# A two-layer hybrid decoder: the first loads go out on two queues, and the last four weight steps take the first 128 tokens ahead of the second 128

## The chip, the cores and the metric

One NeuronCore of one Trainium2 chip runs the whole program. The metric is the time of one execution in microseconds, as the device measures it; the profile of one such execution has a span (first to last instruction) that is a little shorter. Engines are named as the profile names them: PE (TensorE, PEld is its weight loading), DVE (VectorE), ACT (ScalarE), POOL (GpSimd) and SP (SyncE, which here only issues loads and stores). Each engine works through its own list of instructions in order: one that waits for a semaphore holds up all that is behind it on that engine.

## What is computed

The input x is 256 tokens of 1024 features in float32. Two layers follow, and a final norm:

```
for l in range(2):
    h = rms_norm(x, norm_mix_w[l]);  z = h @ w_in[l] + b_in[l]          # 1024 x 5640
    ya = dilated_mixture_attention(rope(aq), rope(ak), av)              # columns of z
    yb = sigmoid(mo) * rms(mlstm(silu(conv(mq, mk)), mv, mi, mf))       # columns of z
    x = x + (sigmoid(ga) * (ya @ w_proj_att[l]) + sigmoid(gb) * (yb @ w_proj_mlstm[l])) @ w_out[l]
    x = x + square(relu(rms_norm(x, norm_mlp_w[l]) @ w_ff1[l])) @ w_ff2[l]
out = rms_norm(x, final_norm_w)
```

## The kernel before, in words

**Weight steps.** All weights are read once, in steps of 256 rows by 512 columns (512 KB). SP loads a step into one of six buffers `raw`. ACT rounds it to a shorter mantissa (`hi`, five buffers), DVE subtracts (`lo` = raw - hi), and PE multiplies activations and weights as three products: low activation by hi, high activation by hi, high activation by lo. The activations are kept the same way, as `slot0h`, `slot0l` (and `slot1h`, `slot1l`). PE results go to eight PSUM tiles `bank`. The products of a step are written either by feature (`by_feature`, 128x256) or by token (`by_token`, 128x512).

**Order.** The program's order is set by a planner when the program is built. Every piece of work is a generator that yields operations; the scheduler (`Scheduler.run`) issues the one that its clock model says can start soonest, with ranks to break ties. In that model (`Plan.now`) an engine and the DMAs that it issues have clocks of their own: `"gps"` and `"gps dma"` are two entries, and a DMA's time is worked out in `Timed` from the second. In the program that comes out, POOL's arithmetic and POOL's DMAs are one list. Nearly every instruction is recorded by one helper line, L199, so that rows are told apart by engine and tile, not by line.

**The start.** `first_loads` issues on SP: the first 128 features of x, the first two weight steps in five pieces, further parts of x, later steps, and the constants `cst`, `bias` and `nw`. x has 256 tokens in two halves t (0 and 1); PE transposes it by pairs of feature blocks, and ACT and DVE split it into `slot0h` and `slot0l`. `first_params` runs on POOL. It issues eight small loads for each layer (`load_params`: norm weights, convolution weights, biases; 92 rows of 128 numbers that land in tile `sg`, buffer `prm[l]`), loads the positions, clears two tiles, and then computes the rotary tables (`rope_tables`). Of these, the last eight POOL operations write `sg` from `ang`, after two sines that ACT computes; PE transposes the result (`ident,sg` 128x128), and ACT copies it to `cos_f` and `sin_f`.

**The parameters.** `columns(l)` has PE transpose the 92 rows of layer l once all eight loads have landed (`ident,sg` 128x92), and DVE copies the result to `col[l]`. It may come at the earliest after weight step 3 for layer 0 and after step 8 for layer 1:

```
def columns(l):
    yield Need((l, "params"), ("step", 3 + 5 * l))
    b, = yield Take(banks)
    yield pe.transpose(b[:, 0:92], prm[l], ident[0:92, 0:92])
```

**The end.** The last four weight steps are rows 3584 to 4095 of `w_ff2`, column half c (0, 1) by row pair kp (0, 1). `out_norm(c)` finishes the output: `plus` adds the product to x (DVE), `total` sums squares (ACT, the last quarter on DVE), POOL takes the power -0.5, `weigh` multiplies by the final norm's weights (DVE), and a scaling and a store follow for each token half. The very last products (second 128 tokens, c = 1) are made in two halves of 256 columns, n = 0 and 1; `Need(tag("total01"))` holds the `plus` of n = 0 until the `weigh` of the second 128 tokens, c = 0, has been issued.

Of the kernel before, what the change touches and what calls it, by code (L numbers as in the profile page):

```python
# [16 lines left out]
P = 128  # L17
S, D, DEPTH, D_IN, D_FF = 256, 1024, 2, 5640, 4096
# [5 lines left out]
N_SPLIT, N_RAW, WARM = 5, 6, (7, 1)  # L24
# [229 lines left out]
class Scheduler:  # L254
# [8 lines left out]
    def add(self, gen, rank=3):  # L263
        self.tasks.append(Task(gen, rank))

    def mark(self, *flags):
        self.done.update(flags)
# [43 lines left out]
def trunk(ctx: ExitStack, tc: tile.TileContext, x_in, positions, norm_mix_w, w_in, b_in, conv_w, conv_b,  # L311
# [9 lines left out]
    act, vec, gps, pe, sync = (Timed(n, e) for n, e in (  # L321
        ("act", nc.scalar), ("vec", nc.vector), ("gps", nc.gpsimd), ("pe", nc.tensor), ("sync", nc.sync)))
    work = Scheduler(plan)
    add, mark = work.add, work.mark
# [14 lines left out]
    raws = [wpool.tile([P, 2, 520], F32, name=f"raw{i}") for i in range(N_RAW)]  # L339
# [4 lines left out]
    ident = one.tile([P, P], F32, name="ident")  # L344
    x = one.tile([P, 2, D], F32, name="x")
# [36 lines left out]
    def rows(w, k0, c0, n):  # L382
        return w.rearrange("(k p) c -> p k c", p=P)[:, k0:k0 + 2, c0:c0 + n]
# [11 lines left out]
    steps = []  # L395
# [6 lines left out]
            yield load(i)  # L402
            mark(("raw", i))

    def load(i, j=slice(0, 2), c=slice(0, None)):
        src, n, _ = steps[i]
        c = slice(c.start, c.stop or n)
        return sync.dma_start(out=raws[i % N_RAW][:, j, c], in_=src[:, j, c])

    def slack(kind):  # L410

# [62 lines left out]
    def token_products(xs, hi, lo, kp, t, o, cs, new, last):  # L474
        xh, xl = xs
        ts = slice(t * P, (t + 1) * P)
        for kt in range(2):
            k = 2 * kp + kt
            yield mm(o, xl[:, k, ts], hi[:, kt, cs], new and kt == 0, False)
            yield mm(o, xh[:, k, ts], hi[:, kt, cs], False, False)  # L480
            yield mm(o, xh[:, k, ts], lo[:, kt, cs], False, last and kt == 1)

    def by_token(w, c0, n, xs, pairs, evac, st=None, begin=True, end=True, k0=0, widths=None, flags=None):

        st = {} if st is None else st
        widths = widths or [n]
        for kp in pairs:
            def fn(i, hi, lo, kp=kp):
                first, last = begin and kp == pairs[0], end and kp == pairs[-1]
                if flags and flags(kp):  # L490
                    yield Need(*flags(kp))
                if first:
                    got = yield Take(banks, 2 * len(widths), KEEP)
                    st["b"] = [got[t * len(widths):(t + 1) * len(widths)] for t in range(2)]
                yield Need(("hi", i), ("lo", i))
                for t in range(2):
                    c = 0
                    for w_i, wd in enumerate(widths):
                        at["part"] = (t * len(widths) + w_i) / (2 * len(widths))
                        bk = st["b"][t][w_i]  # L500
                        yield from token_products(xs, hi, lo, kp, t, bk[:, :wd], slice(c, c + wd), first, last)
                        if last:
                            add(evac(t, w_i, bk), 1)
                        c += wd
            steps.append((rows(w, k0 + 2 * kp, c0, n), n, fn))

    def by_token_last(w, c0, xs, evac, st, k0):

        kept = []

        def first(i, hi, lo):
            kept.append((hi, lo))
            yield Need(("hi", i), ("lo", i))
            yield from token_products(xs, hi, lo, 0, 0, st["b"][0][0], slice(0, 512), False, False)

        def second(i, hi, lo):
            kept.append((hi, lo))
            yield Need(("hi", i), ("lo", i))
            yield from token_products(xs, hi, lo, 1, 0, st["b"][0][0], slice(0, 512), False, True)
            add(evac(0, 0, st["b"][0][0]), 1)  # L520
            extra = yield Take(banks)
            for n, bk in enumerate((st["b"][1][0], extra[0])):
                cs = slice(256 * n, 256 * n + 256)
                for kp in range(2):
                    yield from token_products(xs, *kept[kp], kp, 1, bk[:, cs], cs, n == 1 and kp == 0, kp == 1)
                add(evac(1, n, bk), 1)
        for kp, fn in enumerate((first, second)):
            steps.append((rows(w, k0 + 2 * kp, c0, 512), 512, fn))


    def transpose_x(kp, xs, wcol, js=(0, 1)):
# [105 lines left out]
    def rows128(v, n):  # L637
        return bass.AP(tensor=v.tensor, offset=v.offset, ap=[[P, n], [1, P]])

    def load_params(l):  # L640
        for a, b, v in ((0, 8, norm_mix_w[l]), (8, 16, norm_mlp_w[l]), (16, 48, conv_w[l]), (48, 56, conv_b[l]),
                        (56, 64, b_in[l, MQ:MV]), (64, 80, b_in[l, GA:D_IN]), (80, 84, b_in[l, AV:MQ]),
                        (84, 92, b_in[l, AQ:AV])):
            yield gps.dma_start(out=prm[l][a:b], in_=rows128(v, b - a))
        mark((l, "params"))
# [9 lines left out]
    def layer(l, X, Y):  # L655
# [5 lines left out]
        tag = lambda s: (l, s)  # L661
# [470 lines left out]
            by_feature(w_ff1[l], 512, Y, (kp,), 0, 3, f1, ff_evac(1))  # L1132
        acc = [{}, {}]
        for f in range(8):
            for c in range(2):
                evac = (ff2_evac if l + 1 < DEPTH else out_norm)(c)
                if l + 1 == DEPTH and f == 7 and c == 1:
                    by_token_last(w_ff2[l], 512 * c, hid(f), evac, acc[c], 4 * f)
                else:
                    by_token(w_ff2[l], 512 * c, 512, hid(f), (0, 1), evac, acc[c], begin=f == 0, end=f == 7, k0=4 * f,  # L1140
                             flags=lambda kp, f=f: [tag(f"f{f}{kp}")])
            if f + 2 < 8:
                by_feature(w_ff1[l], 512 * (f + 2), Y, (0, 1, 2, 3), 0, 3, {}, ff_evac(f + 2))

# [7 lines left out]
    xv = x_in.rearrange("o (t p) d -> p (o t) d", p=P)  # L1152
# [22 lines left out]

    def first_loads():

        def load_x(a, b):
            return sync.dma_start(out=x[:, :, a * P:b * P], in_=xv[:, :, a * P:b * P])

        def whole(i):
            yield load(i)
            mark(("raw", i))

        yield load_x(0, 1)
        mark("x0")
        for n, (i, j, c, _) in enumerate(pieces):
            yield load(i, j, c)
            mark(f"piece{n}")
            if n in (1, 3):  # L1190
                a, b = ((1, 2), (2, 4))[n // 2]
                yield load_x(a, b)
                mark(f"x{b - 1}")
        mark(("raw", 0), ("raw", 1))
        for kp in range(1, 4):
            if kp > 1:
                yield load_x(2 * kp, 2 * kp + 2)
                mark(f"x{2 * kp + 1}")
            for i in ((2, 3), (4,), (5,))[kp - 1]:
                yield from whole(i)  # L1200
        yield sync.dma_start(out=cst, in_=consts)
        mark("cst")
        yield from load_bias(0, sync)
        add(loads(N_RAW), 0)

    def first_params():
        yield from load_params(0)
        yield gps.dma_start(out=pos_i, in_=positions.rearrange("o (t p) -> p (o t)", p=P))
        yield from load_params(1)
        yield gps.memset(mv[:, :, :, P:P + 1], 1.0)  # L1210
        yield gps.memset(rot, 0.0)
        yield Need("cst")
        yield from rope_tables(pos_i)

    def first_constants():
        yield act.dma_start(out=ident, in_=eye)
        yield act.dma_start(out=w0, in_=rows128(norm_mix_w[0], 8))
        yield vec.memset(ones, 1.0)
        yield gps.memset(half[:, 0:2], -0.5)

        yield act.activation(mean, half[:, 0:2], AF.Exp)

# [10 lines left out]
                add(i(2), slack("hi" if i is highs else "lo"))  # L1233

    def first_x():
        yield from first_constants()
        yield from warm(WARM[0])
        b, = yield Take(banks)
        yield pe.transpose(b[:, 0:8], w0, ident[0:8, 0:8])
        yield vec.tensor_copy(wcol0, b[:, 0:8])  # L1240
        banks.give(b)
        for j in range(2):
            yield Need(f"x{j}")
            yield from transpose_x(0, X, wcol0, (j,))
            mark(("x", j))
            if j == 0:
                add(warm(WARM[1]), 0)
        mark((-1, "x0"))
        for kp in range(1, 4):
            yield Need(f"x{2 * kp + 1}")  # L1250
            yield from transpose_x(kp, X, wcol0)
            mark((-1, f"x{kp}"))
# [22 lines left out]
    mark(*[(kind, -i) for kind in ("step", "lo") for i in range(1, 10)])  # L1275
    add(first_loads(), 0)
    add(first_params(), 2)
    add(first_x(), 0)
    for n in range(len(pieces)):
        add(first_split(n), 0)  # L1280
    add(first_r(), 2)
# [29 lines left out]
```

## Time and profile before

| | |
|---|---|
| median of 3 runs | 760.55 us (759.99 to 761.11) |
| profiled execution, its time | 759.99 us |
| its span | 758.2 us |
| mean granted TensorE clock | 0.998 |
| PE, DVE, ACT, POOL busy | 99%, 65%, 55%, 7% of the span |

The profiled execution is the fastest of the three runs. Between its time and its span lie 1.8 us that no engine's row shows. A share of 99% is an average; which wait ends last is to be read at the place in the program that a change touches.

### The profile page before, as it was taken

The numbers are of one execution on the slowest core, as the hardware profiler recorded it, in microseconds if no ns is written. First come the engines' busy times: TensorE is split into PE (matmuls) and PEld (weight loads), VectorE is DVE, ScalarE is ACT, GpSimd is POOL, SyncE is SP. The second block draws the span as 40 slices with busy tenths as digits, with TensorE's granted clock in tenths as the row PEclk, the third lists the DMA queues.
The fourth block names the chain that finished last, engine by engine and source line by source line (L and its number), as shares of the span: only waits on it lengthen the run. The fifth ranks groups of instructions, "written<-read, shape, count | busy, mean of one in ns | idle before, by whom it ended". The sixth has DMA issues, their size and how long they took to land.

```text
span 758.2 us, 13079 instructions
## 1 busy us (share of the span) xinstructions
PE 748.6 (99%) x5195; PEld 688.7 (91%) x5195; DVE 492.8 (65%) x751; ACT 417.0 (55%) x659; POOL 55.8 (7%) x106
## 2 busy tenths in 40 slices
PE   8999999999999999999999999999999999999996
PEld 8989889998999988899899898999989899998885
DVE  5898896567664455555569987865866655445553
ACT  6657676445554455554456476755454655445452
POOL 6872010000000000000000000000000000000000
PEclk9999999999999999999999999999999999999999
DMA  9866564556556555555654654445665555655511
GB/s 306 293 194 182 167 182 140 189 177 190 169 175 205 180 189 194 181 184 191 194 169 127 218 165 133 155 161 174 192 207 182 182 185 188 194 182 185 191 56 55
DMA packets 71260, 136.16 MB, mean 180 GB/s; under 512 B 4792, under 2 KB 6752, under 8 KB 71200
## 3 DMA queue, kind: packets, MB, share of 16 engines
q1 hardware_dynamic: 69984, 133.66, 54.6%
q0 software_dynamic: 912, 1.41, 0.7%
q8 instruction: 40, 0.66, 0.3%
q10 hardware_dynamic: 304, 0.27, 0.1%
q14 instruction: 20, 0.16, 0.1%
HBM read 133.74 MB, written 1.05 MB: 178 GB/s over the span
## 4 chain that ended last, share of the span: by engine, by line
PE 97%; DMA 1%; DVE 0%; ACT 0%; SPq 0%; issue 0%; POOLq 0%
PE bank L199 97%; DMA x<-in_x 1%; SPq L199 0%; ACT hi L199 0%; DVE lo L199 0%; DVE x L199 0%; POOLq L1307 0%; ACT sg L199 0%; DVE sg L199 0%; ACT big L199 0%; ACT slot0h L199 0%; DVE big L199 0%; DVE small L199 0%; POOLq L199 0%
## 5 line engine op out<-in xcount | busy, mean ns | idle before, releaser
L199 DVE TENSOR_TENSOR lo<-raw,hi 128x1024 fp32r<-128x1024 f32 (+3 forms) x251 | 304.3, 1214 | 209.8 <-ACT hi L199 209.1
L199 ACT ACTIVATE hi<-raw 128x1024 fp32r<-128x1024 f32 (+3 forms) x251 | 262.5, 1048 | 270.2 <-PE bank L199 247.1
L199 PE MATMUL bank<-slot1h,hi 128*128 128x256 f32 x576 | 162.6, 282 | 0.0
L199 PE MATMUL bank<-slot1h,lo 128*128 128x256 f32 x576 | 162.4, 282 | 0.0
L199 PE MATMUL bank<-slot1l,hi 128*128 128x256 f32 x576 | 162.4, 282 | 0.0
L199 PE MATMUL bank<-slot0h,hi 128*128 128x256 f32 x576 | 161.6, 283 | 0.0
L199 PE MATMUL bank<-slot0h,lo 128*128 128x256 f32 x576 | 160.8, 283 | 0.6 <-DVE lo L199 0.6
L199 PE MATMUL bank<-slot0l,hi 128*128 128x256 f32 x576 | 161.3, 282 | 0.0
L199 PEld LDWEIGHTS bank<-slot1h,hi 128*128 128x128 f32 x576 | 108.4, 188 | 0.8 <-issue 0.3
L199 PEld LDWEIGHTS bank<-slot0l,hi 128*128 128x128 f32 x576 | 107.9, 188 | 1.3 <-issue 0.8
L199 PEld LDWEIGHTS bank<-slot1h,lo 128*128 128x128 f32 x576 | 108.5, 188 | 0.5 <-issue 0.5
L199 PEld LDWEIGHTS bank<-slot1l,hi 128*128 128x128 f32 x576 | 108.3, 188 | 0.5
L199 PEld LDWEIGHTS bank<-slot0h,hi 128*128 128x128 f32 x576 | 107.8, 188 | 0.9 <-issue 0.3
L199 PEld LDWEIGHTS bank<-slot0h,lo 128*128 128x128 f32 x576 | 107.7, 188 | 1.0 <-DVE lo L199 0.8
L199 PE MATMUL bank<-hi,slot1h 128*128 128x512 f32 (+2 forms) x228 | 85.7, 376 | 0.0
L199 PE MATMUL bank<-hi,slot1l 128*128 128x512 f32 (+2 forms) x228 | 85.5, 375 | 0.0
L199 PE MATMUL bank<-lo,slot1h 128*128 128x512 f32 (+2 forms) x228 | 85.5, 375 | 0.0
L199 PE MATMUL bank<-hi,slot0h 128*128 128x512 f32 (+1 forms) x224 | 85.1, 380 | 0.0
L199 PE MATMUL bank<-hi,slot0l 128*128 128x512 f32 (+1 forms) x224 | 84.9, 379 | 0.0
L199 PE MATMUL bank<-lo,slot0h 128*128 128x512 f32 (+1 forms) x224 | 84.9, 379 | 0.0
L199 PEld LDWEIGHTS bank<-lo,slot1h 128*128 128x128 f32 x228 | 42.8, 188 | 8.2
L199 PEld LDWEIGHTS bank<-hi,slot1l 128*128 128x128 f32 x228 | 42.8, 188 | 8.0
(155 smaller groups left out, 719.0 us busy)
## 6 DMA issues: line engine op xcount, KB each, us to landing
raw<-in_w_ff SPq DMA_DIRECT2D x128, 512.0 KB
raw<-in_w_in SPq DMA_DIRECT2D x78, 512.0 KB
raw<-in_w_out SPq DMA_DIRECT2D x16, 512.0 KB
raw<-in_w_in SPq DMA_DIRECT2D x8, 520.0 KB
raw<-in_w_proj_mlstm SPq DMA_DIRECT2D x8, 512.0 KB
raw<-in_w_proj_att SPq DMA_DIRECT2D x8, 512.0 KB
raw<-in_w_in SPq DMA_DIRECT2D x3, 256.0 KB
x<-in_x SPq DMA_DIRECT2D x3, 256.0 KB
```

The lines of the kernel that those rows point to most:

```text
L199: f(*args, **kw)
```

## The change

Four things are changed in the text of the program.

1. The first loads are issued on SP and on ACT. ACT issues the identity, `w0`, the second 128 features of x and the third weight piece; SP issues the rest, with the third part of x behind the fifth piece.
2. The small constants have a task of their own, whose table-loading activation waits for the third piece's load to be issued. The later parts of x (`other_x`) get a task of rank 1.
3. In `first_params`, `load_params(1)` is moved from ahead of the rotary tables to behind them.
4. In the last four weight steps, both column halves of the first 128 tokens are multiplied before the second 128 tokens.

```diff
-    def load(i, j=slice(0, 2), c=slice(0, None)):
+    def load(i, j=slice(0, 2), c=slice(0, None), queue=None):
...
-        return sync.dma_start(out=raws[i % N_RAW][:, j, c], in_=src[:, j, c])
+        return (queue or sync).dma_start(out=raws[i % N_RAW][:, j, c], in_=src[:, j, c])
...
-    def by_token_last(w, c0, xs, evac, st, k0):
+    def by_token_last(w, xs, evacs, acc, k0, flags):
...
+            first, second = (acc[c]["b"][t][0] for t in range(2))
+            yield from token_products(xs, hi, lo, kp, 0, first, slice(0, 512), False, kp == 1)
+            if kp:
+                add(evacs[c](0, 0, first), 1)
+            if len(kept) < 4:
+                return
+            for kp in range(2):
+                yield from token_products(xs, *kept[kp], kp, 1, acc[0]["b"][1][0], slice(0, 512), False, kp == 1)
+            add(evacs[0](1, 0, acc[0]["b"][1][0]), 1)
             extra = yield Take(banks)
-            for n, bk in enumerate((st["b"][1][0], extra[0])):
+            for n, bk in enumerate((second, extra[0])):
...
+        yield act.dma_start(out=ident, in_=eye)
         yield load_x(0, 1)
         mark("x0")
         for n, (i, j, c, _) in enumerate(pieces):
-            yield load(i, j, c)
+            if n == 2:
+                yield act.dma_start(out=w0, in_=rows128(norm_mix_w[0], 8))
+                mark("w0")
+                yield load_x(1, 2, act)
+                mark("x1")
+            yield load(i, j, c, act if n == 2 else sync)
             mark(f"piece{n}")
-            if n in (1, 3):
-                a, b = ((1, 2), (2, 4))[n // 2]
-                yield load_x(a, b)
-                mark(f"x{b - 1}")
         mark(("raw", 0), ("raw", 1))
         for kp in range(1, 4):
-            if kp > 1:
-                yield load_x(2 * kp, 2 * kp + 2)
-                mark(f"x{2 * kp + 1}")
+            yield load_x(2 * kp, 2 * kp + 2)
+            mark(f"x{2 * kp + 1}")
...
     def first_params():
         yield from load_params(0)
         yield gps.dma_start(out=pos_i, in_=positions.rearrange("o (t p) -> p (o t)", p=P))
-        yield from load_params(1)
         yield gps.memset(mv[:, :, :, P:P + 1], 1.0)
         yield gps.memset(rot, 0.0)
         yield Need("cst")
         yield from rope_tables(pos_i)
+        yield from load_params(1)
 
     def first_constants():
-        yield act.dma_start(out=ident, in_=eye)
-        yield act.dma_start(out=w0, in_=rows128(norm_mix_w[0], 8))
...
+        yield Need("piece2")
```

**POOL.** The list of POOL before, around the positions' load; `sg` is the tile in which the parameters of both layers land (the second eight loads are layer 1):

```order
L199 DMA sg_123<-in_b_in 8x128
L199 DMA pos_i<-in_positions 128x2x1
L199 DMA sg_123<-in_norm_mix_w 8x128
L199 DMA sg_123<-in_norm_mlp_w 8x128
L199 DMA sg_123<-in_conv_w 32x128
L199 DMA sg_123<-in_conv_b 8x128
L199 DMA sg_123<-in_b_in 8x128
L199 DMA sg_123<-in_b_in 16x128
L199 DMA sg_123<-in_b_in 4x128
L199 DMA sg_123<-in_b_in 8x128
L199 MEMSET mv 128x8
```

The list of POOL after, from the last two writes of the rotary tables (`sg_124<-ang`) on:

```order
L199 TENSOR_SCALAR sg_124<-ang_280 128x2x8
L199 COPY sg_124<-ang_280 128x2x8
L199 DMA sg_123<-in_norm_mix_w 8x128 [waits DMASW1_49]
L199 DMA sg_123<-in_norm_mlp_w 8x128 [waits DMASW2_49]
L199 DMA sg_123<-in_conv_w 32x128 [waits DMASW3_49]
L199 DMA sg_123<-in_conv_b 8x128 [waits DMASW4_49]
L199 DMA sg_123<-in_b_in 8x128 [waits DMASW5_49]
L199 DMA sg_123<-in_b_in 16x128 [waits DMASW6_49]
L199 DMA sg_123<-in_b_in 4x128 [waits DMASW7_49]
L199 DMA sg_123<-in_b_in 8x128
```

The eight loads of layer 1 have moved from the 16th to 23rd place of POOL's list to the 90th to 97th, behind the whole of the rotary tables.

**PE, the transposes that read these tiles.** Before, the transpose of layer 1's parameters (`ident,sg_123` 128x92) stands between products of the gate columns of layer 0, some 200 rows ahead of the transposes of the rotary tables:

```order
L199 MATMUL bank_71<-hi_102,slot0h 128x260
L199 MATMUL bank_71<-lo_107,slot0h 128x260
L199 MATMUL bank_72<-ident,sg_123 128x92 [waits DMASW4_49,DMASW3_49,DMASW5_49,DMASW2_49,DMASW6_49,DMASW1_49,DMASW7_49,DMASW0_49,DVE_49]
L199 MATMUL bank_70<-hi_103,slot0l 128x260 [waits Activation_49]
L199 MATMUL bank_70<-hi_103,slot0h 128x260
```

After, it stands in the weight step `hi_103` of the attention's query columns, behind the transposes of the rotary tables (`ident,sg_124`) and those of a gate (`ident,small`):

```order
L199 MATMUL bank_66<-slot0l,hi_103 128x256
L199 MATMUL bank_68<-ident,sg_124 128x128 [waits Pool_49] x4
L199 MATMUL bank_66<-slot0h,lo_108 128x256
L199 MATMUL bank_66<-slot0h,hi_103 128x256
L199 MATMUL bank_69<-ident,small 4x128 [waits DVE_49]
L199 MATMUL bank_69<-ident,small 4x128
L199 MATMUL bank_66<-slot0l,hi_103 128x256
L199 MATMUL bank_66<-slot0h,lo_108 128x256
L199 MATMUL bank_66<-slot0h,hi_103 128x256
L199 MATMUL bank_66<-slot0l,hi_103 128x256
L199 MATMUL bank_66<-slot0h,lo_108 128x256
L199 MATMUL bank_71<-ident,sg_123 128x92 [waits DMASW4_49,DMASW5_49,DMASW3_49,DMASW6_49,DMASW2_49,DMASW7_49,DMASW1_49,DMASW0_49]
```

Between the transposes of the rotary tables and that of the parameters there are now seven products and one pair of small transposes; the semaphores `DMASW0` to `DMASW7` are those of POOL's loads.

On ACT, the table load ahead of the two sines of `ang` now stands right behind the rounding of `raw_96` to `hi_100`; before, a copy of `bank_70` and a tanh (`big_77<-mqk`) stood between them, of which the tanh now comes ahead of that rounding and the copy behind the sines.

**DVE at the end.** Before, with `x` as the sum, `small` the sums of squares and `sg_124<-x,sg_123` the weighing; `bank_73` holds the second 128 tokens of c = 0, `bank_70` the first 128 of c = 1, `bank_67` and `bank_68` the second 128 of c = 1:

```order
L199 SCALAR_TENSOR_TENSOR x<-bank_73,small,x 128x512 [waits PE_49]
L199 TENSOR_SCALAR small<-small 128x1 [waits Activation_49]
L199 TENSOR_TENSOR sg_124<-x,sg_123 128x512 [waits DMASW3_49,DVE_49]
L199 TENSOR_SCALAR small<-small 128x1 [waits Activation_49]
L199 TENSOR_TENSOR sg_124<-x,sg_123 128x512 [waits DVE_49]
L199 SCALAR_TENSOR_TENSOR x<-bank_70,small,x 128x512 [waits PE_49]
L199 SCALAR_TENSOR_TENSOR x<-bank_67,small,x 128x512 [waits PE_49]
L199 SCALAR_TENSOR_TENSOR small<-small 128x1 [waits Activation_49]
L199 TENSOR_TENSOR sg_124<-x,sg_123 128x512 [waits DVE_49]
L199 SCALAR_TENSOR_TENSOR x<-bank_68,small,x 128x256 [waits DVE_49,PE_49]
```

After, where `bank_73` holds the first 128 tokens of c = 1, `bank_71` the second 128 of c = 0, and `bank_67` and `bank_72` the second 128 of c = 1:

```order
L199 SCALAR_TENSOR_TENSOR x<-bank_73,small,x 128x512 [waits PE_49]
L199 SCALAR_TENSOR_TENSOR small<-small 128x1 [waits Activation_49]
L199 TENSOR_TENSOR sg_124<-x,sg_123 128x512 [waits DVE_49]
L199 SCALAR_TENSOR_TENSOR x<-bank_71,small,x 128x512 [waits PE_49]
L199 TENSOR_SCALAR small<-small 128x1 [waits Activation_49]
L199 TENSOR_TENSOR sg_124<-x,sg_123 128x512 [waits DVE_49]
L199 SCALAR_TENSOR_TENSOR x<-bank_67,small,x 128x512 [waits PE_49]
L199 SCALAR_TENSOR_TENSOR x<-bank_72,small,x 128x256 [waits DVE_49,PE_49]
L199 SCALAR_TENSOR_TENSOR small<-small 128x1 [waits Activation_49]
L199 ISA big_74,small<-x,small 128x256 [waits DVE_49]
```

The sum of the second 128 tokens over c = 0 and its weighing came ahead of the first 128 tokens of c = 1; now they come behind, and ahead of the last two sums.

## Rows read from the trace of the kernel before

**Rows 1.** The page: engines' busy time, and the chain that ended last by engine.

```profile
PE 748.6 (99%) x5195; PEld 688.7 (91%) x5195; DVE 492.8 (65%) x751; ACT 417.0 (55%) x659; POOL 55.8 (7%) x106
PE 97%; DMA 1%; DVE 0%; ACT 0%; SPq 0%; issue 0%; POOLq 0%
```

**Rows 2.** PE's waits over the span: us in total, times, longest.

```profile
...
PE bank L199 <- DMA x<-in_x: 0.9, 2, 0.6
PE bank L199 <- DVE lo L199: 0.6, 1, 0.6
```

**Rows 3.** Stretch 20 to 100: PE, PEld, DVE, ACT, POOL busy, PEclk, DMA share, GB/s.

```profile
20.00:100.00 80.00, 80.00 (x581) 74.59 (x580) 70.61 (x147) 52.93 (x104) 36.72 (x70) 1.00 0.65 206
```

**Rows 4.** Timeline of ACT, 57 to 62: start, us, operation [idle <-releaser].

```profile
57.46 1.06 ACT L199 ACTIVATE hi<-raw 128x1024 fp32r<-128x1024 f32 x1 [1.88 <-PE bank L199]
...
60.28 1.28 ACT L199 ACT_TABLE_LOAD   x1
61.58 0.32 ACT L199 ACTIVATE ang<-ang 128x16 f32<-128x16 f32 x2
```

**Rows 5.** Timeline of POOL, 58 to 66: the tables' last writes.

```profile
61.95 0.61 POOL L199 TENSOR_SCALAR sg<-ang 128x16 f32<-128x16 f32 x1 [7.68 <-ACT ang L199]
...
63.02 1.23 POOL L199 TENSOR_SCALAR sg<-ang 128x16 f32<-128x16 f32 x1
...
64.62 0.20 POOL L199 COPY sg<-ang 128x16 f32<-128x16 f32 x1
```

**Rows 6.** Tile sg on POOL, 1 to 12.4: the parameter loads, ns min/median/max.

```profile
L199 POOL DMA_DIRECT2D sg<-in_b_in x8: 498/505/517, 3.5 to 11.9; - x8
L199 POOL DMA_DIRECT2D sg<-in_norm_mix_w x2: 515/616/717, 1.2 to 6.3; - x2
...
DMA to landing us min/median/max: 2.6/4.9/6.1
```

**Rows 7.** Timeline of PE, 60 to 67: step `hi_103` and the table transposes.

```profile
63.91 0.28 PE L199 MATMUL bank<-slot0h,hi 128*128 128x256 f32 x1
64.03 0.28 PE L199 MATMUL bank<-slot0l,hi 128*128 128x256 f32 x1
...
64.87 0.60 PE L199 MATMUL bank<-ident,sg 128*128 128x128 f32 x4
65.22 0.36 PE L199 MATMUL bank<-slot0h,lo 128*128 128x256 f32 x1
```

**Rows 8.** Two stretches, 66 to 72: engines, PEclk, DMA share, GB/s.

```profile
66.00:68.00 2.00, 2.00 (x18) 1.87 (x17) 1.22 (x4) 1.17 (x4) 0.00 (x0) 1.00 0.99 314
...
70.00:72.00 2.00, 2.00 (x20) 2.00 (x19) 1.29 (x2) 2.00 (x4) 0.57 (x1) 1.00 0.00 0
```

**Rows 9.** A stretch of the end: PE busy, PEclk, DMA share, GB/s.

```profile
755.00:755.50 0.50, 0.00 (x0) 0.50 0.99 389
```

**Rows 10.** The product of `ones` on PE, 0 to 4.2 and 4.6 to 5.1.

```profile
L199 PE MATMUL bank<-ones 128*128 128x128 f32 x14 | 3.2, 424 | 1.0 <-DVE ones L199 1.0
L199 PE MATMUL bank<-ones 128*128 128x128 f32 x2 | 0.4, 275 | 0.0
```

**Rows 11.** Timeline of the end, without PE's earlier rows.

```profile
748.36 0.75 DVE L199 SCALAR_TENSOR_TENSOR x<-bank,small,x 128x512 f32<-128x512 f32 x1 [0.49 <-PE bank L199]
749.14 0.63 ACT L199 ACTIVATE big<-x 128x512 f32<-128x512 f32 x1 [2.07 <-DVE x L199]
...
750.50 0.69 DVE L199 TENSOR_TENSOR sg<-x,sg 128x512 f32<-128x512 f32 x1
...
750.87 0.28 PE L199 MATMUL bank<-lo,slot1h 128*128 128x256 f32 x1
...
751.19 0.48 DVE L199 SCALAR_TENSOR_TENSOR x<-bank,small,x 128x256 f32<-128x256 f32 x1
...
751.65 1.15 ACT L199 ACTIVATE sg<-sg,small 128x1024 f32<-128x1024 f32 x1 [0.53 <-POOL small L199]
...
752.41 0.86 POOL L199 TENSOR_TENSOR small<-small,half 128x1 f32<-128x1 f32 x1 [0.79 <-DVE small L199]
```

More of the change, by code (lines that the diff above doesn't have):

```diff
@@ L505, in by_token, with fn @@
             steps.append((rows(w, k0 + 2 * kp, c0, n), n, fn))
-    def by_token_last(w, c0, xs, evac, st, k0):
+    def by_token_last(w, xs, evacs, acc, k0, flags):
         kept = []
-        def first(i, hi, lo):
+        def fn(i, hi, lo):
+            c, kp = divmod(len(kept), 2)
             kept.append((hi, lo))
+            if c == 0:
+                yield Need(*flags(kp))
             yield Need(("hi", i), ("lo", i))
[L514 to L520, printed above, removed]
+            first, second = (acc[c]["b"][t][0] for t in range(2))
[7 more added lines that the diff above has]
+            add(evacs[0](1, 0, acc[0]["b"][1][0]), 1)
             extra = yield Take(banks)
-            for n, bk in enumerate((st["b"][1][0], extra[0])):
+            for n, bk in enumerate((second, extra[0])):
                 cs = slice(256 * n, 256 * n + 256)
                 for kp in range(2):
[L525 to L528, printed above, removed]
+                    yield from token_products(xs, *kept[2 + kp], kp, 1, bk[:, cs], cs, n == 1 and kp == 0, kp == 1)
+                add(evacs[1](1, n, bk), 1)
+        for c in range(2):
+            for kp in range(2):
+                steps.append((rows(w, k0 + 2 * kp, 512 * c, 512), 512, fn))
     def transpose_x(kp, xs, wcol, js=(0, 1)):
@@ L1134, in layer @@
         for f in range(8):
+            fl = lambda kp, f=f: [tag(f"f{f}{kp}")]
+            if l + 1 == DEPTH and f == 7:
+                by_token_last(w_ff2[l], hid(f), [out_norm(c) for c in range(2)], acc, 4 * f, fl)
+                continue
             for c in range(2):
[L1136 to L1141, printed above, removed]
+                by_token(w_ff2[l], 512 * c, 512, hid(f), (0, 1), ff2_evac(c), acc[c], begin=f == 0, end=f == 7,
+                         k0=4 * f, flags=fl)
             if f + 2 < 8:
@@ L1176, in first_loads, with load_x @@
     def first_loads():
-        def load_x(a, b):
-            return sync.dma_start(out=x[:, :, a * P:b * P], in_=xv[:, :, a * P:b * P])
+        def load_x(a, b, queue=sync):
+            return queue.dma_start(out=x[:, :, a * P:b * P], in_=xv[:, :, a * P:b * P])
         def whole(i):
@@ L1235, in first_x @@
     def first_x():
-        yield from first_constants()
         yield from warm(WARM[0])
         b, = yield Take(banks)
+        yield Need("w0")
         yield pe.transpose(b[:, 0:8], w0, ident[0:8, 0:8])
@@ L1248, in first_x, with other_x @@
         mark((-1, "x0"))
+    def other_x():
+        yield Need((-1, "x0"))
         for kp in range(1, 4):
@@ L1277, in trunk @@
     add(first_params(), 2)
+    add(first_constants(), 0)
     add(first_x(), 0)
+    add(other_x(), 1)
     for n in range(len(pieces)):
```

## The prediction, written before the changed kernel ran

> **What bounds the kernel now.** I read the page first, for the engine that sets the end: PE is busy for 99% of the span and makes up 97% of the chain that ended last, while DVE, ACT and POOL have slack [rows 1]. So a microsecond in which PE stands still is a microsecond of the kernel, and one of another engine counts only where PE waits for it. Then PE's waits: once its first tile is there, it waited 0.9 for x and 0.6 for a lo [rows 2], which is at the start; over the 80 us from 20 to 100 it is busy for 80.00 [rows 3]. Whatever the change mends at the start is worth at most the 1.5 us of the last two waits; whatever wait it puts into the middle is paid in full, since there is none for it to hide behind. So I read the order of the changed program for places where PE meets something that now comes later, and then the timelines of ACT, POOL and PE around that place.
>
> **The moved loads.** The eight loads of layer 1's parameters used to go out on POOL between 6 and 12 us [rows 6]. Now they stand behind the rotary tables. In the planner's clock POOL's DMAs run beside POOL's arithmetic, so it takes the loads to be long landed and puts their reader, the 128x92 transpose, on PE seven products and a small pair behind the transposes of the tables. On the chip POOL is one list, and the transpose waits for all eight. Both ends of this race can be worked out.
>
> When the loads land. The tables' last eight POOL operations wait for two sines on ACT. Before, the rounding of `hi_100` ends at 57.46 + 1.06 = 58.52, but the table load starts only at 60.28, behind two operations that the new order takes out of the way; the sines end at 61.90 [rows 4]. Now the table load can start at 58.54, so that the sines end 60.28 - 58.54 = 1.74 earlier, at 60.16. POOL's eight operations took from 61.95 to 64.82, 2.87 us with one of 1.23 in them [rows 5]; now they end at about 63.0. Then come the loads: 0.62 for the first, about 0.51 for each of the others [rows 6], so the eighth starts 0.62 + 6 x 0.51 = 3.7 later, at 66.7. From its issue to its landing a load took 2.6 to 6.1 us, median 4.9 [rows 6]. The median is from the start, when the DMA engines were full; from 66 to 68 they are at 0.99 again, from 70 to 72 at 0.00 [rows 8]. So I take 4.2, between the shortest and the median, nearer to the latter: landing at 70.9.
>
> When PE is there. Step `hi_103` began at 63.91 [rows 7]. Ahead of it the new order has one transpose of parameters and the pair `ident,small` less, three at the 0.09 of the tables' four (64.87 to 65.22, 0.35), so 63.6. Then those four transposes, nine products at 0.12 each (63.91 to 64.03) and the pair, 0.2 with what it delays [rows 7]: 63.6 + 0.35 + 1.1 + 0.2 = 65.2. At the tables' transposes, 63.85, the tables are done at 63.0, so there is no wait. At the 128x92 transpose PE waits from 65.2 to 70.9, **5.7 us**. Queued behind it on PE is everything else. ACT and DVE can only go on until their five buffers are full, and DVE soon stops too, at the copy to `col` that waits for this transpose. POOL's next work, a broadcast, needs DVE. So all is shifted, and nothing is given back.
>
> Bounds of the stall. Shortest: tables in 1.9 (the 1.23 at the 0.25 of its like), landing in 2.6: 60.2 + 1.9 + 3.7 + 2.6 = 68.4, a stall of 3.2. Longest: sines as late as before, 61.9, landing in 6.1: 61.9 + 2.9 + 3.7 + 6.1 = 74.6, a stall of 9.4.
>
> Here a page of the Trainium skill speaks, "DMA: Bandwidth & Descriptors", in the section "Anatomy of one DMA — SWDGE (gpsimd) path": a DMA that GpSimd issues has a fixed cost of about 2.0 us, nearly all of it until the last byte is confirmed. By that the eighth would land at 68.7, an estimate, the stall would be 3.5 in place of 5.7, and the sum would lie in rival 1. The trace does not agree: no load of rows 6 was that quick, and the sum goes by the rows.
>
> **The clock.** PE's last product starts at 750.87 and ends at 751.15 [rows 11]. After that PE is idle, and from 755.0 to 755.5 the granted clock reads 0.50 [rows 9]: it fell to 1.2 GHz within that idle stretch. The stall of 5.7 us is a like stretch, so I expect a fall in it. What getting back costs can be read at the start. There 14 products of `ones` took 3.2 us, one each (3.2 - 0.42) / 13 = 0.21; two later ones came 0.12 apart [rows 10]. The first 14 thus ran at about half pace, whatever clock is on record there, and lost 14 x 0.09 = **1.3 us**. Below, this is zero if the clock holds; above, I know no row that shows a longer recovery.
>
> **The first loads.** What is removed: x's second block is issued a slot earlier, on ACT, and its third block is no longer waited for ahead of the second step's products. At most this gives back 1.5 us, the two waits [rows 2]. What is added: ACT's in-order list now has the rounding of the third weight step ahead of the second x pair, so `slot0h` of that pair waits for a 512 KB load; and the second x block goes ahead of the second weight piece on ACT and DVE, some 0.3 later for that piece. The loss is at most about the 0.6 of the wait for lo, met again one operation earlier. I take -0.2, with -1.5 and +0.6 as ends.
>
> **The end.** The first 128 tokens are finished 12 products earlier, but the last chain hangs on the second 128 tokens, and their products end at 751.15 as before. DVE now has to add the second 128 tokens of c = 0 at 748.36 to 749.11, and ACT squares them only behind the scaling of the first 128, 1.15 long [rows 11], whose power is now ready that early; I estimate its start at 748.3. So the square of 0.63 runs from 749.45, not 749.14, to 750.1 [rows 11]; with some 0.25 for reading its sum out and adding it, the weighing of 0.69 ends at 751.0, and only then, by the `Need`, comes the sum of n = 0 with its 0.75 [rows 11], to 751.7. The sum of n = 1, which starts at 751.19 now, as PE releases it, starts at 751.7, 0.5 later [rows 11], and ACT's square between the two is late too. The last power, at 752.41 before [rows 11], starts some 0.6 later. Against it the store of the first 128 tokens is out of the way of the last two. I take +0.2, with -0.5 and +0.6 as ends.
>
> **The sum**, against the profiled execution's own 759.99: 5.7 (stall) + 1.3 (clock) - 0.2 (start) + 0.2 (end) = 7.0, so 767.0. The median of the runs shown is 0.56 above that execution; between 767.0 and 767.6 I give **767.3 us**.
>
> **Rivals.**
> 1. The stall is there but the clock holds, or the load lands nearer to 2.6 than to 4.9 with the queues empty. Then 3.2 to 5.7 and no 1.3: 763.2 to 765.7. For it: the DMA engines at 0.00 from 70 on [rows 8]. Against it: an idle stretch on PE as long as that of the end.
> 2. POOL is slower than I think: the sines stay where they were, or the loads' issue stretches. One POOL operation of the tables took 1.23 in place of 0.25 [rows 5]. Against it: the issues of rows 6 took 498 to 717 ns with DVE at work. A stall of 7.7 to 9.4 and the clock give 769 to 770.7. The Trainium skill, "SBUF — State Buffer", section "SBUF: two separate sides", speaks for this rival: GpSimd cannot write a load's descriptors while certain DVE operations hold the shared port.
> 3. Not slower: the loads land before PE asks. This is one race at one place, the 128x92 transpose, and is decided where the eighth load lands by 65.2. With the shortest landing and tables that needs sines that end by 65.2 - 2.6 - 3.7 - 1.9 = 57.0, before `hi_100` is rounded. Against it stand all the rows; for it only that the order might not tell what POOL can overlap. Then start and end are left: 760.0, and with the ends' best bounds 758.0.
>
> **How the numbers follow.** Forecast (stall and clock, 765.5 to 769) 0.55; rival 1, 0.28; rival 2, 0.12; rival 3, 0.05, of which 0.02 falls below 759.0. Faster or slower by over 0.2%, 1.5 us, is about what the runs' own spread (759.99 to 761.11) lets one tell. The range leaves out rival 3, the quickest tenth of rival 1 and the longest stalls: 763.3 to 770. Faster 0.02, same 0.04, slower 0.94.
>
> **What would show it.** In the changed kernel's profile PE's waits gain one of 5 to 6 us for a POOL load of `sg`, near 65 us; POOL's timeline has eight loads at about 63 to 67; the granted clock reads 0.50 somewhere between 68 and 75; products there are 0.22 apart. PE's waits for x are gone or smaller. At the end the first scaling by ACT stands near 748.3 plus the shift, and the last power starts about 1.9 after PE's last product, not 1.3. I am wrong if PE has no such wait, if the loads are issued before the tables end, or if another wait of PE over 1 us stands elsewhere in the middle.

## The result, and the profile after

The changed kernel takes **769.36 us** (median of 6 executions, 766.76 to 770.05) beside 760.52 us of the kernel before in the same measurement (6 executions, 759.99 to 761.11): a ratio of 1.011, 95% interval 1.0096 to 1.0125. It is slower by 8.8 us. The forecast was 767.3 in a range of 763.3 to 770.0. The execution that was profiled is the quickest of the six: 766.76 us, span 765.0, mean granted clock 0.994. The other five lie at 768.6 to 770.05, and why is part of what follows.

PE's waits in the changed kernel, in the columns of [rows 2] (us in total, times, longest):

```profile
PE bank L199 <- DMA sg<-in_b_in: 5.2, 1, 5.2
...
PE bank L199 <- DMA x<-in_x: 0.8, 1, 0.8
PE bank L199 <- ACT hi L199: 0.4, 1, 0.4
```

One new wait, for a POOL load of `sg`; those of the start are 1.2 us in place of 1.5. The timeline of the changed kernel around it (all engines, the rows that count), to be held against [rows 4, 5, 7]:

```profile
57.41 0.63 ACT L199 ACTIVATE big<-mqk 128x512 f32<-128x512 f32 x1 [2.03 <-DVE mqk L199]
...
57.95 1.05 ACT L199 ACTIVATE hi<-raw 128x1024 fp32r<-128x1024 f32 x1
...
59.01 1.28 ACT L199 ACT_TABLE_LOAD   x1
...
59.26 3.57 DVE L199 TENSOR_TENSOR lo<-raw,hi 128x1024 fp32r<-128x1024 f32 x3
...
60.30 0.32 ACT L199 ACTIVATE ang<-ang 128x16 f32<-128x16 f32 x2
...
60.67 1.05 POOL L199 TENSOR_SCALAR sg<-ang 128x16 f32<-128x16 f32 x1 [4.71 <-ACT ang L199]
...
61.68 1.21 POOL L199 COPY sg<-ang 128x16 f32<-128x16 f32 x1
...
63.74 0.60 PE L199 MATMUL bank<-ident,sg 128*128 128x128 f32 x4
63.74 0.20 POOL L199 COPY sg<-ang 128x16 f32<-128x16 f32 x1
63.88 0.68 POOL L199 DMA_DIRECT2D sg<-in_norm_mix_w  x1
...
66.09 2.02 POOL L199 DMA_DIRECT2D sg<-in_b_in  x4
70.62 0.41 PE L199 MATMUL bank<-ident,sg 92*128 92x92 f32 x1 [5.23 <-DMA sg<-in_b_in]
```

Read it from the bottom: PE stood for 5.23 us, from 65.39, in front of the 128x92 transpose. The four loads of `b_in` took 2.02 us to issue, so the eighth began at 66.09 + 3 x 0.505 = 67.6, and PE went on 3.0 later. The first load went out when the tables' last write was done (63.74 + 0.20, and 63.88; POOL's rows are rough by that much).

Behind the wait PE is slow. Stretches of the changed kernel (columns as in [rows 8]):

```profile
70.00:71.00 1.00, 0.38 (x2) 0.38 (x3) 0.00 (x0) 0.00 (x0) 0.00 (x0) 0.60 0.00 0
71.00:72.00 1.00, 1.00 (x7) 1.00 (x7) 0.23 (x1) 0.00 (x0) 0.00 (x0) 0.50 0.06 16
72.00:73.00 1.00, 1.00 (x6) 1.00 (x6) 0.99 (x4) 0.51 (x2) 0.00 (x0) 0.50 0.00 0
...
74.00:75.00 1.00, 1.00 (x11) 1.00 (x10) 0.69 (x1) 0.99 (x2) 0.00 (x0) 1.00 0.01 3
```

The clock fell to 0.50 (1.2 GHz) in the wait: six or seven matmuls a microsecond in place of eleven. Thirteen products take from 70.75 to 73.65, 2.90 us, where 13 x 0.119 = 1.55 would do at the full clock: 1.35 lost.

The end, timeline of the changed kernel, to be held against [rows 11]:

```profile
754.73 1.15 ACT L199 ACTIVATE sg<-sg,small 128x1024 f32<-128x1024 f32 x1 [1.26 <-POOL small L199]
...
755.78 0.61 ACT L199 ACTIVATE big<-x 128x512 f32<-128x512 f32 x1
...
756.59 0.68 DVE L199 TENSOR_TENSOR sg<-x,sg 128x512 f32<-128x512 f32 x1
...
757.19 1.33 DVE L199 SCALAR_TENSOR_TENSOR x<-bank,small,x 128x512 f32<-128x512 f32 x2
757.26 0.28 PE L199 MATMUL bank<-lo,slot1h 128*128 128x256 f32 x1
...
759.40 0.86 POOL L199 TENSOR_TENSOR small<-small,half 128x1 f32<-128x1 f32 x1 [4.71 <-DVE small L199]
```

ACT scales the first 128 tokens (754.73) and squares the others only then (755.78); DVE's weighing (756.59) follows, and both last sums (757.19) behind it. The last power starts 759.40 - 757.26 = 2.14 behind the start of PE's last product, before 752.41 - 750.87 = 1.54. To the end of the span it is 765.0 - 757.26 = 7.7, before 758.2 - 750.87 = 7.3: 0.4 more (the spans are given to 0.1).

So in this execution: 6.8 (the spans' difference) = 5.23 (wait) + 1.35 (clock) + 0.4 (end) - 0.2 (what is left, put down to the start).

### The profile page after: what moved, and what is told of

Its sections match the earlier page's. It is cut to its first block, busy times and chain, and to the rows that moved or that the text cites. A ratio compares the mean times of both kernels' runs of the same rounds, so it can differ in the third digit from the quotient of the medians.

```text
span 765.0 us, 13079 instructions
## 1 busy us (share of the span) xinstructions
PE 750.0 (98%) x5195; PEld 690.4 (90%) x5195; DVE 491.9 (64%) x750; ACT 417.4 (55%) x660; POOL 58.4 (8%) x106
## 3 DMA queue, kind: packets, MB, share of 16 engines
HBM read 133.74 MB, written 1.05 MB: 176 GB/s over the span
## 4 chain that ended last, share of the span: by engine, by line
PE 96%; DMA 1%; POOL 1%; ACT 1%; DVE 0%; issue 0%; ACTq 0%; POOLq 0%
PE bank L199 96%; POOL sg L199 1%; DMA x<-in_x 1%; DMA sg<-in_b_in 0%; ACT big L199 0%; ACT sg L199 0%; DVE x L199 0%; ACTq L199 0%; POOLq L1318 0%; POOL small L199 0%; DVE sg L199 0%; DVE small L199 0%; DVE big L199 0%; ACT slot0h L199 0%; ACT hi L199 0%
```

## The experiments

**1. The same again.** The changed kernel, no edit.

> The changed kernel once more, unchanged, for a second trace. Its profiled execution took 766.76 us at a mean granted clock of 0.994, the five others 768.6 to 770.05 at 0.990 to 0.993. My theory: the others stall as long (5.2 us, give or take 0.3), but TensorE stays at 1.2 GHz some 6 us longer afterwards, so the profile shows 0.50 over some 9 us in the middle in place of 3. Rival: the clock is a by-product, and the eighth load lands some 2.5 us later in those executions, a stall of 7.5 to 8. Median 769.4 either way.

769.73 us (4 executions), ratio 1.0115 (1.0097 to 1.0133); the profiled one took 768.99, span 767.2, clock 0.990. PE's waits in it:

```profile
PE bank L199 <- DMA sg<-in_b_in: 5.6, 1, 5.6
PE bank L199 <- DMA x<-in_x: 1.4, 1, 1.4
```

Its tables' transposes start at 65.41, in the first trace at 63.74. So 1.67 of the 2.2 us between the two executions had been lost before the stall. A mark for the start is the transpose of layer 0's parameters, which is PE's 130th instruction in every kernel here. Its rows in the kernel before, the changed kernel, `again` and `loads_alone` (experiment 7), in this order:

```profile
20.11 0.24 PE L199 MATMUL bank<-ident,sg 92*128 92x92 f32 x1
20.01 0.24 PE L199 MATMUL bank<-ident,sg 92*128 92x92 f32 x1
21.68 0.24 PE L199 MATMUL bank<-ident,sg 92*128 92x92 f32 x1
22.96 0.24 PE L199 MATMUL bank<-ident,sg 92*128 92x92 f32 x1
```

The 1.67 were lost before 21.68, at the start. Neither explanation put down for this run is it: the stall is only 0.4 longer, and what follows it costs 0.2 more. The clock did stay at 0.50 for longer, from 69 to 76, but about half of that lay inside the wait:

```profile
69.00:70.00 1.00, 0.00 (x0) 0.00 (x0) 0.00 (x0) 0.00 (x0) 0.78 (x2) 0.61 0.79 208
...
76.00:77.00 1.00, 1.00 (x10) 1.00 (x10) 0.68 (x1) 0.76 (x1) 0.00 (x0) 0.98 0.00 1
```

What happened at the start is in its stretches there:

```profile
7.00:8.00 1.00, 0.61 (x6) 0.40 (x4) 0.45 (x2) 0.95 (x3) 0.28 (x1) 0.89 1.02 328
8.00:9.00 1.00, 1.00 (x5) 1.00 (x6) 0.99 (x4) 1.00 (x3) 0.00 (x0) 0.50 1.02 383
...
10.00:11.00 1.00, 1.00 (x6) 1.00 (x6) 0.27 (x1) 1.00 (x1) 0.17 (x1) 0.50 1.04 371
11.00:12.00 1.00, 1.00 (x10) 1.00 (x9) 0.93 (x1) 0.04 (x1) 0.01 (x1) 0.90 1.10 387
```

After a wait of 1.4 us for x, the clock is at 0.50 for three microseconds. The five other executions of the first measurement have no trace, so that this is shown for one execution only.

**2 and 3. The moved loads back, and moved alone.** `params_first` is the changed kernel, `late_alone` the kernel before, with this line at the other place:

```diff
 def first_params():
     yield from load_params(0)
     yield gps.dma_start(out=pos_i, ...)
+    yield from load_params(1)      # params_first; late_alone: the reverse
...
     yield from rope_tables(pos_i)
-    yield from load_params(1)
```

> The changed kernel with layer 1's parameter loads put back ahead of the rotary tables; the new first loads and the new end stay. My theory: no wait of PE between 20 and 750 us, the clock never falls there, and what is left of the change is the start (-0.3) and the end (+0.4): 760.3 to 760.9, against 760.5 before. Rival: the new first loads or the new end cost more than the trace lets see and the move of the loads less: 762 or more.

> The kernel before, with only layer 1's parameter loads moved behind the rotary tables. My theory: the whole loss is here: a stall of 5 to 6 us at the 128x92 transpose, the clock at 0.50 behind it, 768 to 770. Rival: the old first loads bring PE there later or POOL to the tables earlier, and the stall is under 3: 764 or less.

`params_first`: 761.81 us beside 760.75, ratio 1.0006 (0.9997 to 1.0015); no wait of PE behind the start, but one of 2.1 for x in it. `late_alone`: 767.97 us (0.03 under its range), ratio 1.0087 (1.0072 to 1.0101), a wait of 5.9. So the move of the loads is most of the loss, 7.2 of 8.8 us. `params_first` came out 0.9 above its range, though: start and end cost about 1 us together between medians, 0.5 by the ratio, and its interval leaves 1 in. In `late_alone` the clock stayed down longer behind the wait:

```profile
71.00:74.00 3.00, 2.90 (x13) 2.66 (x14) 1.02 (x3) 1.23 (x3) 0.00 (x0) 0.50 0.02 5
74.00:77.00 3.00, 3.00 (x16) 3.00 (x16) 1.53 (x3) 2.99 (x6) 1.30 (x1) 0.50 0.00 0
77.00:78.00 1.00, 1.00 (x10) 1.00 (x8) 0.55 (x2) 0.87 (x1) 0.00 (x0) 0.87 0.00 0
```

That is six microseconds at half pace: 13 + 16 matmuls in 2.90 + 3.00 us of work, where 29 x 0.119 = 3.5 would do, some 2.4 lost. The changed kernel's first trace has 1.35 behind a wait of 5.2: the price of nearly the same stall is not one number.

**4 and 5. The reader later.** The changed kernel with the 128x92 transpose asked for at step 20 (`column_mid`) or step 22 (`column_later`); the loads stay behind the tables.

```diff
-        yield Need((l, "params"), ("step", 3 + 5 * l))
+        yield Need((l, "params"), ("step", 3 + 17 * l))    # column_later: 19
```

> The changed kernel with layer 1's 128x92 transpose asked for at step 22 in place of step 8, which puts it 92 rows later on PE, some 11 us; the loads stay behind the tables. My theory: it is a race, and the loads (landing near 70.6) now win it, so no stall: 760.3 to 760.9. Rival: late loads cost something on their own, by POOL's queue (the broadcast of mu, the tables) or by the DMA rings: 762 or more.

> The changed kernel with the 128x92 transpose asked for at step 20, 40 rows later on PE, some 4.8 us. My theory: the stall shrinks to 0.4 to 0.8 us and the clock does not fall over so short a wait: 760.8 to 761.6. Rival: any wait of PE in the middle costs the clock too: 762 to 764.

`column_later`: 761.77 us, ratio 1.0009 (0.9999 to 1.0019); PE waits for no `sg`, and the time is that of `params_first` (761.81). So it is a race: late loads as such cost nothing that these runs can tell. Its time missed the range by 0.9, as that of `params_first` did, which has the same start and end. `column_mid`: 762.28 us beside 760.63, ratio 1.0019 (1.0009 to 1.0028), with a wait of 1.5 where 0.4 to 0.8 was expected. Its timeline and stretches:

```profile
66.33 2.02 POOL L199 DMA_DIRECT2D sg<-in_b_in  x4
...
72.16 0.27 PE L199 MATMUL bank<-ident,sg 92*128 92x92 f32 x1 [1.50 <-DMA sg<-in_b_in]
```

```profile
71.00:72.00 1.00, 0.00 (x0) 0.00 (x0) 0.00 (x0) 1.00 (x2) 0.00 (x0) 1.00 0.28 41
72.00:73.00 1.00, 0.84 (x7) 0.88 (x8) 0.54 (x2) 0.89 (x1) 0.00 (x0) 1.00 0.76 141
73.00:74.00 1.00, 1.00 (x11) 1.00 (x10) 1.00 (x3) 0.00 (x0) 0.00 (x0) 1.00 0.99 377
```

The eighth load began at 66.33 + 1.51 = 67.85 and PE got it 4.3 later, not 3.0: the median of [rows 6] was nearer here than in the stalled kernels. Over a wait of 1.50 the clock stayed at 1.00. The measured time lies in the rival's range, but its mechanism, a fall of the clock, isn't in this trace.

**6. Four of the eight loads moved.**

```diff
...
+    yield from load_params(1, slice(0, 4))
...
     yield from rope_tables(pos_i)
-    yield from load_params(1)
+    yield from load_params(1, slice(4, 8))
```

> The changed kernel with four of the eight loads put back ahead of the tables, so that four are issued behind them, some 2.1 us less of POOL; PE's order is that of the changed kernel. My theory: the stall is set by the issue of the loads and shrinks to 3.1 us, and the clock still falls: 764.7 to 767.5. Rival 1: the clock holds over so short a stall: 763.4 to 763.9. Rival 2: landing is set by something else, and the stall stays near 5.2: 767 or more.

766.57 us, ratio 1.0076 (1.0061 to 1.0091): in my range. The wait is 3.8, not 3.1 (the last load began at 66.77, and PE went on 3.65 later), and the clock fell just behind it: it reads 0.50 from 72 to 74. In this trace everything before the stall stands 1.2 later (the tables' transposes at 64.94, not 63.74), so the last load is 2 us earlier against the rest, and that bought 1.4 of stall.

**7 and 8. The start alone, the end alone.** The kernel before with items 1 and 2 of the change (`loads_alone`), or with item 4 (`tail_alone`).

> The kernel before with the new first loads alone; layer 1's parameter loads stay ahead of the tables, and the end is the old one. My theory: -0.3 from the waits at the start (1.5 us of PE before, 1.2 in the changed kernel, and small work moved): 760.0 to 760.4. Rival: the waits saved count in full, 759.0; or the start is slower, 761 or more.

> The kernel before with the new order of the last four weight steps alone. My theory: from the start of PE's last product to the end of the span it takes 7.7 in place of 7.3 us, since the last chain on DVE is late: 760.7 to 761.1. Rival: the early store pays, 760.3 or less.

`loads_alone`: 761.36 us beside 760.63, ratio 1.0003 (0.9993 to 1.0012); `tail_alone`: 761.14 (0.04 above its range), ratio 1.0007 (0.9998 to 1.0015). Neither interval leaves 1 out, so the times show neither loss; the traces show both. The traced execution of `loads_alone` is the slowest of its eleven (762.73). The start in `loads_alone`, timeline of PE, and a stretch of it:

```profile
7.34 0.69 PE L199 MATMUL bank<-ident,x 128*128 128x128 f32 x2 [1.70 <-DMA x<-in_x]
...
11.19 0.63 PE L199 MATMUL bank<-slot0l,hi 128*128 128x256 f32 x2
11.62 0.63 PE L199 MATMUL bank<-slot0h,hi 128*128 128x256 f32 x2
12.05 0.63 PE L199 MATMUL bank<-slot0l,hi 128*128 128x256 f32 x2
12.47 0.82 PE L199 MATMUL bank<-slot0h,lo 128*128 128x256 f32 x4
13.13 0.40 PE L199 MATMUL bank<-slot0h,hi 128*128 128x256 f32 x2
```

```profile
11.00:13.00 2.00, 2.00 (x11) 2.00 (x11) 1.51 (x2) 0.53 (x1) 2.00 (x5) 1.00 1.07 374
```

PE waits 1.70 for x's second block; two products take 0.43 up to 12.47, so the 24 products before 13.13 lose some 2.6 us (5.46 from 7.67 to 13.13, where 24 x 0.118 = 2.83 would do). PE's last product starts at 753.57, before at 750.87. The median lies in the range of the rival "slower", and this trace has its mechanism. In `tail_alone` it is 759.3 - 751.61 = 7.69 us from PE's last product to the end: the forecast 7.7.

**9 and 10. Which load is late at the start.** `loads_alone` with x's second block back on SP, or with the third weight piece back there:

```diff
-                yield load_x(1, 2, act)
+                yield load_x(1, 2)                # x_on_sp
...
-            yield load(i, j, c, act if n == 2 else sync)
+            yield load(i, j, c)                   # piece_on_sp
```

> The kernel before with the new first loads, but x's second block issued on SP behind the first two weight pieces, where it was, and the third piece on ACT. With x's second block on ACT the runs so far show PE waiting 0.85 to 2.05 us for it, and products at half pace behind the wait. My theory: the loss of the start is this one load, which lands later though it is issued earlier; back on SP the wait is under 0.6, half pace ends by 9 us, and the time is 759.9 to 760.5. Rival: five weight pieces ahead of everything fill the DMA engines, and x's block is late on either queue: 761.0 to 761.6.

> The kernel before with the new first loads, but the third weight piece on SP again, so that ACT issues only the identity, the norm weights and x's second block. Theory A, the block is late because ACT's queue gets a small share of the DMA engines beside SP's: the wait stays 0.8 to 2.0 us and the time 761.0 to 761.6. Theory B, the piece on ACT's own queue is what holds it up: the wait falls under 0.6, and the time is 759.9 to 760.5.

`x_on_sp`: 760.57 us beside 760.85, ratio 0.9994 (0.9985 to 1.0002), a wait of 0.8, above the 0.6 expected. `piece_on_sp`: 761.03, ratio 1.0002 (0.9992 to 1.0011), a wait of 1.7, as theory A has it. The times don't tell these apart, and one trace each is little. `both_mended` (below), whose first loads are those of `x_on_sp`, shows 2.1:

```profile
PE bank L199 <- DMA x<-in_x: 2.1, 1, 2.1
```

So my theory of this one load on this one queue falls; that the block can be late on either queue, as the rival had it, is what the traces of `x_on_sp` and `both_mended` show, though the time of `x_on_sp` is not in the rival's range. What stands over all traces: with either load on ACT's queue PE waited 0.8 to 2.1 us for the second block (ten traces); with both on SP at most 0.34 (the kernel before, `tail_alone`, `mended_alone`, `late_alone`).

**11 and 12. The end mended, and both.** `mended_alone` is `tail_alone` with the sum of n = 0 held only until the squares of c = 0 are issued, the weighing of the second 128 tokens behind that sum, and the scaling of the first 128 behind that square; `both_mended` has the first loads of `x_on_sp` too.

```diff
...
-                    yield from weigh(t, c0, c0 + 512)
-                    mark(tag(f"total{c}{t}"))
+                    if t == 1:
+                        mark(tag("total01"))
+                    else:
+                        add(weigh_first(c), 1)
...
                     yield from plus(1, bk, 512, D)
                     mark("first")
+                    add(weigh_second(), 1)
...
-                yield Need(tag("total10"))
+                yield Need(tag("total10"), tag("total00"), tag("total01"))
```

> The kernel before with the new end, in which the sum of the second 128 tokens' first 256 of c = 1 no longer stands behind the weighing of their c = 0 half on DVE, and ACT squares that half ahead of scaling the first 128 tokens. From the start of PE's last product to the end of the span: 7.3 us before, 7.7 in the changed kernel. My theory: that order was the loss of the end: 7.0 to 7.3 us here, 760.1 to 760.7. Rival: the store or PE's order is the loss, and the end stays at 7.6 or more: 760.9 to 761.3.

> Both mended parts together: the new first loads with x's second block back on SP, the new end with its order on DVE and ACT mended, and layer 1's parameter loads ahead of the tables as before. Singly they stood at 760.57 and 760.39 beside 760.85 of the kernel before. If the gains add, 0.3 and 0.5 under the kernel before: 759.8 to 760.3 where that shows 760.6 to 760.9. Rival: both were noise, since neither interval leaves 1 out, and the two are level: 760.5 or more.

`mended_alone`: 760.39 us beside 760.85, ratio 0.9995 (0.9987 to 1.0004). From PE's last product to the end of its span it is 758.5 - 751.33 = 7.17 us, before 7.3 and in `tail_alone` 7.69, so the loss of the end was the order on DVE and ACT; which of the three edits to it counts was not tried. `both_mended`: 760.46 beside 760.87, ratio 0.9992 (0.9983 to 1.0001), the end at 759.6 - 752.47 = 7.13 us, but the start as above. The time lies between the two ranges, so that the runs don't say whether the gains add; no version here is shown to beat the kernel before.

## Why the prediction was right, and where it was off

**The stall** (5.7 forecast; 5.23 and 5.64 in the changed kernel, 5.91 in `late_alone`) is right by place and cause. That the size is so near is partly luck: of its steps two were off and nearly made up for each other. The tables' end was forecast at 63.0 and came at 63.9. Half a microsecond of that is the rounding of `hi_100`, which began at 57.95, not 57.46: the tanh now stands ahead of it on ACT (57.41, 0.63 long), as the order shown with the change says, and the sum left it out. The rest is that of the tables' eight operations two took over 1 us (1.05 and 1.21), not one; both lie beside DVE's three subtractions in a row (59.26 to 62.83). The landing was forecast at 4.2 and took 3.0, 3.4, 3.0 and 3.65 in the four stalled traces. PE was there at 65.39 (65.2 forecast), the release at 70.62 (70.9). The 2.0 us of the Trainium skill, "DMA: Bandwidth & Descriptors", section "Anatomy of one DMA — SWDGE (gpsimd) path", don't agree with the traces here: the quickest of these landings took 3.0.

**The clock** (1.3 forecast): 1.35 and some 1.5 in the two traces of the changed kernel, 2.4 in `late_alone`. The top end, "no row that shows a longer recovery", was too low. Rival 1 was half right: the landing did come nearer to 2.6 than to 4.9, which alone would have brought the stall down to some 4.5. But the tables were late, and the clock did not hold: it fell in or just behind every stall, down to the one of 3.8 us.

**The end** (+0.2 forecast, up to +0.6): +0.4, by the steps as they were told. The first scaling stands at 754.73; less the 6.39 by which PE's last product is later, that is 748.34 (748.3 forecast). The last power is 0.6 later. The early store gives back about 0.2 (from the last scaling to the end of the span 4.70, before 4.89), half of what I had netted against it.

**The start** (-0.2 forecast, at most +0.6) is the step that failed; that the profiled execution agrees with it is luck. The other trace of the changed kernel has -0.2 + 1.67 = +1.5. `loads_alone` has 2.7 in its trace, 0.7 between medians and 0.2 by the ratio, whose interval leaves 1 in. Layer 0's parameter transpose, the mark of experiment 1, stands at 19.69 to 20.61 in the four traces with the old first loads and at 20.01 to 22.96 in the ten with new ones. I took an earlier issue for an earlier landing: the second block of x was issued at 1.79 on ACT, not at 2.21 on SP, yet over the eight traces in which ACT issues it PE got it between 6.40 and 7.34, where it came between 5.34 (the first wait for x in [rows 2]) and 5.81 with the old first loads. And I had a clock term for the stall only, where behind a wait at the start the products can be slow too. They are not always: behind the same wait of 0.8 us PE counts 10 or 11 matmuls from 8 to 9 us in the changed kernel and in `column_mid`, 5 and 7 in `four_moved` and `x_on_sp`. The median lies 769.36 - 767.3 = 2.1 above the forecast. In `again`, whose time is near the median, the start is the largest piece of that; between medians start and end make up some 1.2 of it, and the rest is not placed. Why the block is late stays open: the DMA engines are at 0.94 to 1.07 from 5 to 6 us in these eight traces, but at 1.05 in the kernel before too. The Trainium skill says in "DMA: Bandwidth & Descriptors", section "Queues, rings and completion order", that a DMA engine takes turns between the queues that have work; no run here shows the order of the packets.

**Do the parts add?** Between medians: 7.2 (`late_alone`) + 0.7 (`loads_alone`) + 0.5 (`tail_alone`) = 8.4, measured 8.8; the intervals of the two small parts leave either at nothing. The median, 769.36, lies just above the forecast's own 765.5 to 769 and in rival 2's 769 to 770.7, so the time alone would speak for rival 2. The traces don't: it needs a stall of 7.7 to 9.4, and they have none over 5.9; two tables' operations were slow, as it feared, but the loads' issues took 0.51 to 0.68 each, no more than in [rows 6]. Rival 3 falls with the stall.

## What to carry to other kernels

A planner that gives an engine's arithmetic and its DMAs separate clocks will put a reader in front of loads that haven't been issued: after each move of a load, look up what stands ahead of it in the real list of the engine that issues it, and where its first reader stands. Price a stall of TensorE with the slow products behind it, as a range, and ask the same of stalls at the start. A load issued earlier on another queue did not land earlier here: look at when its reader gets it, over more than one execution.

## What the hardware showed that was not expected

- The clock record says 1.00 in `loads_alone` from 11 to 13 us, where the row counts 11 matmuls in 2 us, products 0.21 apart. At the start of the program the pace of the products tells more than the recorded clock.
- Nearly the same stall is followed by 2.9 us of half pace (changed kernel) or by 6 (`late_alone`). A wait of 1.50 us at 71 left the clock at 1.00, one of 3.8 did not; but one of 1.4 at the start was followed by 0.50 from 8 to 11 us (`again`).
- The tables' last eight POOL operations are four of one kind and four of another, all on 128x16 numbers. Two took 1.05 and 1.21 us, the six others 0.19 to 0.25, in both traces of the changed kernel. The slow ones ended at 61.72 and 62.89 in the first, beside DVE's three subtractions without a break (59.26 to 62.83), and the quick ones came behind them. In the kernel before, the one of 1.23 (63.02 to 64.25, [rows 5]) lies beside a subtraction from 62.89 to 64.14. That DVE holds POOL up is what this looks like; no run here tried it.
